# A gated delta rule's state update: contraction over a unit's 128 rows with keys set to nought in the other chunk's rows, instead of over the chunk's own 64 rows

## The chip, the cores and the metric

The kernel runs on one core of one Trainium2 chip, as one program with one launch. The metric is the device time in microseconds. Matrix products run on TensorE (PE in the profile; its weight loads are a row of their own, PEld), elementwise work on VectorE (DVE), ScalarE (ACT) and GpSimd (POOL); SyncE (SP) issues the DMAs.

## The reference

Two layers of a decoder trunk over 1024 tokens with 1024 channels. Each layer normalises its input, projects it once, feeds three token mixers that read the same projection, gates each branch, and adds an output projection to the input. A last RMS norm follows. Only the first mixer is touched here: the gated delta rule with 4 heads of 128 channels in chunks of 64 tokens.

```
def step(state, inp):
    q_n, k_n, u_n, w_n, g_n, a_n = inp
    v_new = u_n - einsum('bhck,bhkv->bhcv', w_n, state)
    o = einsum('bhck,bhkv->bhcv', q_n * exp(g_n)[..., None], state) + einsum('bhij,bhjv->bhiv', a_n, v_new)
    g_last = g_n[..., -1]
    state = state * exp(g_last)[..., None, None] + einsum(
        'bhck,bhcv->bhkv', k_n * exp(g_last[..., None] - g_n)[..., None], v_new)
    return state, o
```

The last einsum, the state update, contracts over the tokens c of one chunk (64 of them). The keys in it are decayed by exp(g_last - g).

The other two mixers are a latent attention with 8 heads and a gated linear recurrence (RG-LRU) of 512 channels.

## The kernel before

The work of a layer has three stages. In the first (phase_a) the input projection is done column tile by column tile: in_tile loads a weight block of 128x1024, splits it into an exact high and low part (wst, whi by DVE on L111, wlo by POOL on L112), and does 48 products of 128x512 with them (L121, L122, L123), into a PSUM tile pbig. Beside these products runs the delta rule. The second stage is the RG-LRU and the first half of the output projection, the third is the attention and the other half.

The delta rule works on two pairs of heads, one after the other, so that there are four scans in all (two layers by two pairs). The tokens of a pair stand in eight units of 128, and a unit holds two chunks, one in partitions 0 to 63 and one in 64 to 127. Four quads of four (unit, head) matrices are prepared (gdn_prep, products on L415, L421, L426, L434) and then scanned (gdn_scan). For each chunk the scan does, in this order: the products of the state S with w and q for both heads (L459, into the PSUM tile pS), the new values vn = uu - pS (DVE, L92, 64 rows), the products of the decayed keys kd with vn for both heads (L463, into pD), and the new state for both heads (DVE, L89, tile S). A copy of pS's other rows (ACT, L466) keeps q's part. At the end of a unit come the products of the decayed attention with vn for both heads (L471). All these are plain float32, and each such product is two records on PE and two on PEld, so that a chunk's L463, with two heads, is four records. There are 2 x 2 x 8 x 2 = 64 chunks, 64 visits to L463.

The line L463 takes only the chunk's own rows of kd and vn (`mine`, 64 of 128), so that its matmul uses 64 rows of the array; the profile marks it 64*128. Everything else in the scan is 128*128. The attention has one other 64*128 product, L749.

The keys kd are made in gdn_prep by POOL, one instruction of 128x128 per (unit, head), from ktok and a column of dec (L412, which the profile books on the helper's line L95). dec holds exp(g_last - g) per token, each row with its own chunk's g_last. kd has two buffers of 128x512, one per quad. POOL works in order and also makes bk, bv and wlo.

A scheduler sets the order of the instructions on each engine from the order of the program, priorities and its own model of durations. in_tile's products have a low priority: they fill the gaps of the scan. An engine then works strictly through that order.

Of the kernel before, what the change touches and what calls it, by code (L numbers as in the profile page):

```python
# [9 lines left out]
F32 = mybir.dt.float32  # L10
# [7 lines left out]
L = 2  # L18
# [4 lines left out]
# Columns of a layer's parameter tile [128, NPAR].  # L23
# [15 lines left out]
# Columns of the constant tile [128, NCON].  # L39
# [10 lines left out]
# Indices of the input projection's column tiles.  # L50
# [13 lines left out]
class Trunk:  # L64
# [7 lines left out]
    @contextmanager  # L72
    def prio(self, d):
        """Instructions that the scheduler prefers less (d > 0) or more (d < 0)."""
        self.tc.cur_priority += d
        yield
        self.tc.cur_priority -= d
# [19 lines left out]
    def load_w(self, src, nk, cols, eng=None, pool=None):  # L97
        """A float32 weight block [128, nk, cols] as its exact float32r parts."""
# [17 lines left out]
    def mm3(self, out, pairs):  # L116
        """out = sum over (ah, al, bh, bl) of a.T @ b, each in three float32r products."""
# [7 lines left out]
    def split(self, hi, lo, x, eng=None):  # L125
        """x as exact float32r parts: hi is x rounded, lo the rest."""
        self.nc.scalar.copy(hi, x)  # L127
        (eng or self.nc.vector).tensor_tensor(lo, x, hi.bitcast(F32), ALU.subtract)  # L128

# [1 line left out]
    def in_tile(self, l, *ms):  # L131
        """The first of the column tiles ms; the others wait for their call. All by halves of the tokens."""
# [13 lines left out]
    def conv(self, y, p, w, bias=None):  # L146
        """Causal depthwise conv of width 4 along the free axis, from PSUM."""
# [7 lines left out]
    def silu2(self, out, z):  # L155
        """out = 2 silu(z), as z (1 + tanh(z / 2))."""
        self.act(out, z, AF.Tanh, scale=0.5)
        self.stt(out, out, 1.0, z, ALU.add, ALU.mult)
# [5 lines left out]
    def newton(self, r, x):  # L164
        """One Newton step of r towards x ** -0.5; x is overwritten."""
# [5 lines left out]
    def add_squares(self, alloc, acc, x, eng):  # L171
        """acc + x * x (acc is None at first)"""
# [7 lines left out]
    def rms_bcast(self, alloc, accs, n, ch, tag, fine=False):  # L180
        """1 / sqrt(mean of squares + eps), on every partition, from the sum of accs over their channels."""
        nc = self.nc
        r = alloc("rb")
        if not fine:
            # brings Ln's table in while the sums are still under way
# [15 lines left out]
    def norm_half(self, alloc, xs, accs, n, gain, tag, share=False):  # L201
        """h = rmsnorm(x) for one half of the tokens, into self.hh, self.hl."""
# [12 lines left out]
    def gates(self, l):  # L215
# [16 lines left out]
        # beside them the RG-LRU's parameters  # L232
# [22 lines left out]
        dec = pa.tile([128, 32], F32, name="dec")  # L255
        for c in range(2):
            q = slice(64 * c, 64 * c + 64)
            self.tt(dec[q], gs[q, 32 + 32 * c : 64 + 32 * c], gc[q], ALU.subtract)
        self.act(dec, dec, AF.Exp)
# [10 lines left out]
    def gdn_qkv(self, l, pr, kind, hd, P):  # L270
# [22 lines left out]
        # squared norms of q, columns (unit, head)  # L293
# [7 lines left out]
    def combos(self, q):  # L301
        """The four (unit, head) of quad q: index, unit, head of the pair, columns."""
        return [(c, 2 * q + c // 2, c % 2, slice(c * 128, c * 128 + 128)) for c in range(4)]

    def gdn_tok(self, pr, P):
        """k and v by token, and the pair's factors per token."""
# [14 lines left out]
        # inverse norms: 1 / sqrt(sum + eps), of vectors that are twice the reference's  # L321
# [9 lines left out]
        # v is held doubled  # L331
# [7 lines left out]
    def gdn_pre(self, pr, P, q):  # L339
        """-A and the decayed attention of one quad; the diagonal blocks go out by DRAM."""  # L340
# [31 lines left out]
    def blocks(self, dram, b):  # L372
        """Diagonal block b (32 x 32) of each of a pair's sixteen 128 x 128 matrices."""
        return bass.AP(dram.tensor, dram.offset + b * (32 * 2048 + 32), [[128, 16], [2048, 32], [1, 32]])

    def gdn_inverse(self, pr):
        """(I + A)^-1 of the 32 x 32 diagonal blocks, one block per partition, and its transpose."""
# [18 lines left out]
    def gdn_prep(self, pr, P, q):  # L396
        """The quad's triangular inverse, applied to v and k."""
# [8 lines left out]
        kd = pa.tile([128, H2], F32, name="kd", tag="kd", bufs=2)  # L406
        for c, u, hd, cs in self.combos(q):
# [4 lines left out]
            self.gts(kd[:, cs], P["ktok"][q][:, cs], self.dec[:, gj : gj + 1])  # L412
# [14 lines left out]
        for hd in range(2):  # L427
            # w of a unit's two chunks around that unit's q
# [10 lines left out]
    def gdn_scan(self, pr, P, q):  # L439
        nc, pa = self.nc, self.pa  # L440
        if q == 0:
            P["S"] = [pa.tile([128, 128], F32, name="S", tag="S", bufs=4) for _ in range(2)]
            for s in P["S"]:
                nc.gpsimd.memset(s, 0.0)
        S, uu, kd = P["S"], P["u"][q], P["kd"][q]
        # the output takes the place of the decayed attention
        o = P["attn"][q]
        for ul in range(2):
            u = 2 * q + ul
            vn = pa.tile([128, 256], F32, name="vn", tag="vn", bufs=2)  # L450
            oq = pa.tile([128, 256], F32, name="qs", tag="qs", bufs=2)
            for par in range(2):
# [8 lines left out]
                for hd, cs, gj in hs:  # L461
                    cq = slice((ul * 2 + hd) * 128, (ul * 2 + hd) * 128 + 128)
                    nc.tensor.matmul(pD[:, cs], kd[mine, cq], vn[mine, cs], start=True, stop=True)  # L463
# [13 lines left out]
    def gdn_norm(self, pr, P):  # L477
        """The output's RMS norm, its gate and its way out; q's inverse norm and 128^-0.5 with them."""
# [31 lines left out]
    def gate_tile(self, l, m, dst, z=None):  # L510
        """2 silu of a column tile, to DRAM"""
# [7 lines left out]
    def lru(self, l):  # L519
        nc, pa, par = self.nc, self.pa, self.par  # L520
        st, res = [], []
        for m in range(4):
# [22 lines left out]
            # 1 - a^2 = tanh(-log a) (1 + a^2)  # L545
# [112 lines left out]
    def rope(self, x, n, s):  # L658
        """Rotary embedding of one half of the tokens; x may be in PSUM."""
# [13 lines left out]
    def attn_q_rope(self, l, pr, res):  # L673
        """q's rotary part of two heads: parts stacked as [hi; lo] per head."""
# [30 lines left out]
    def attn_v(self, l, pr, V):  # L705
        """v of two heads: per two token blocks, [128, (block, head, 128)]."""
# [470 lines left out]
```

## Time and profile before

| | |
|---|---|
| median of three runs | 2239.93 us (2239.56, 2239.93, 2247.45) |
| profiled execution, first to last instruction | 2240.5 us |
| PE busy | 2143.5 us (96%), 10380 records |
| DVE, ACT, POOL busy | 1321.0, 880.7, 705.6 us |
| granted TensorE clock, mean | 0.984 of full |

The profile is of one execution. Besides the span of its instructions it gives no second time for that execution; the span stands 0.6 us above the median of the runs, so that the two can be compared directly. Busy times of PE are unions of pipelined records, whose ends are modelled: what a product costs is read from the distance between starts, not from its duration.

### The profile page before, as it was taken

How to read it: one execution, taken by the hardware profiler on the slowest of the kernel's cores; microseconds unless marked ns; L12 is line 12 of the kernel's file. 1: busy time of each engine (PE TensorE's matmuls, PEld its weight loads, DVE VectorE, ACT ScalarE, POOL GpSimd, SP SyncE). 2: the span in 40 equal slices, each digit the busy share in tenths (PEclk: the TensorE clock that was granted, in tenths of full speed). 3: DMA queues.
4: the chain of work that ended last, by engine and by line, in shares of the span. 5: the costliest groups of instructions: out<-in, count | busy, mean ns of one | idle time of the engine just before them, and what ended most of it. 6: DMA issues, size and time to landing. Idle time of an engine off the chain costs nothing. (4 is left out here: it accounts for less than half of the span.)

```text
span 2240.5 us, 28710 instructions
## 1 busy us (share of the span) xinstructions
PE 2143.5 (96%) x10380; PEld 1695.7 (76%) x10380; DVE 1321.0 (59%) x2496; ACT 880.7 (39%) x1784; POOL 705.6 (31%) x712
## 2 busy tenths in 40 slices
PE   7999999999899999999989999999998999999997
PEld 4788877787677777777668888788777877777774
DVE  6546547545833766666664575483467247666666
ACT  5241254135611544443533313522375025443535
POOL 3222222323632333232242222322336323232322
PEclk9999999999999999999999999999999999999999
DMA  4223113412253024326321331134213520325172
GB/s 149 71 78 111 53 57 99 135 41 85 94 186 100 20 79 143 122 88 198 129 78 38 109 97 36 57 99 128 72 60 122 169 82 30 121 88 175 43 226 99
DMA packets 135101, 222.06 MB, mean 99 GB/s; under 512 B 37808, under 2 KB 60336, under 8 KB 134960
## 3 DMA queue, kind: packets, MB, share of 16 engines
q1 hardware_dynamic: 134960, 220.24, 30.6%
q8 instruction: 82, 1.34, 0.3%
q14 instruction: 59, 0.48, 0.1%
HBM read 147.31 MB, written 72.88 MB: 98 GB/s over the span
## 5 line engine op out<-in xcount | busy, mean ns | idle before, releaser
L112 POOL TENSOR_TENSOR wlo<-wst,whi 128x1024 fp32r<-128x1024 f32 (+3 forms) x196 | 316.2, 1614 | 903.6 <-DVE whi L111 308.8
L121 PE MATMUL pbig<-h,whi 128*128 128x512 f32 x1216 | 486.4, 400 | 9.2 <-ACT h L127 6.2
L123 PE MATMUL pbig<-h,wlo 128*128 128x512 f32 x1216 | 486.5, 400 | 4.0 <-POOL wlo L112 4.0
L122 PE MATMUL pbig<-h,whi 128*128 128x512 f32 x1216 | 485.8, 399 | 2.1 <-DVE h L128 1.0
L121 PEld LDWEIGHTS pbig<-h,whi 128*128 128x128 f32 x1216 | 231.7, 191 | 56.6 <-ACT h L127 7.0
L123 PEld LDWEIGHTS pbig<-h,wlo 128*128 128x128 f32 x1216 | 231.7, 191 | 50.8 <-POOL wlo L112 5.3
L122 PEld LDWEIGHTS pbig<-h,whi 128*128 128x128 f32 x1216 | 231.4, 190 | 50.2 <-POOL h L128 3.3
L86 ACT ACTIVATE P<-pS,mx,scq 128x512 f32<-128x512 f32 (+1 forms) x192 | 128.1, 671 | 158.9 <-DVE mx L89 88.2
L111 DVE CAST whi<-wst 128x1024 fp32r<-128x1024 f32 x92 | 76.9, 836 | 150.2 <-PE pbig L122 118.4
L95 POOL TENSOR_SCALAR P<-P,mx 128x128 f32<-128x128 f32 (+6 forms) x112 | 80.6, 720 | 231.0 <-DVE mx L766 186.9
L109 ACT CAST whi<-wst 128x256 fp32r<-128x256 f32 (+2 forms) x104 | 46.3, 447 | 231.3 <-DMA wst<-in_w_uq 105.2
L127 ACT CAST pth<-pstp 128x512 fp32r<-128x512 f32 x192 | 91.3, 479 | 93.2 <-PE pstp L795 93.2
L755 DVE TENSOR_REDUCE mx<-pS 128x1 f32<-128x512 f32 (+1 forms) x192 | 106.6, 555 | 24.3 <-PE pS L749 17.1
L128 DVE TENSOR_TENSOR ptl<-pstp,pth 128x512 fp32r<-128x512 f32 x192 | 105.1, 554 | 23.9 <-ACT pth L127 23.2
L86 ACT ACT_TABLE_LOAD x81 | 103.9, 1283 | 2.4 <-PEq L1169 0.7
L795 PE MATMUL pstp<-con,P 128*128 128x128 f32 x576 | 98.7, 278 | 3.4 <-DVE P L770 3.4
L121 PE MATMUL pspj<-lh,whi 128*128 128x512 f32 x208 | 88.1, 424 | 6.1 <-DVE k L128 5.5
L92 DVE TENSOR_TENSOR xt<-pspj,xt 128x512 f32<-128x512 f32 x96 | 66.3, 690 | 46.7 <-PE pspj L123 40.8
L795 PEld LDWEIGHTS pstp<-con,P 128*128 128x128 f32 x576 | 71.2, 141 | 25.0 <-DVE P L770 4.8
L749 PE MATMUL pS<-kl,qr 64*128 64x512 f32 (+1 forms) x192 | 85.1, 443 | 0.0
L123 PE MATMUL pspj<-lh,wlo 128*128 128x512 f32 x208 | 82.4, 396 | 0.6 <-POOL wlo L112 0.6
L122 PE MATMUL pspj<-ll,whi 128*128 128x512 f32 x208 | 82.4, 396 | 0.0
(267 smaller groups left out, 4565.5 us busy)
## 6 DMA issues: line engine op xcount, KB each, us to landing
wst<-in_w_in SPq DMA_DIRECT2D x76, 512.0 KB, 3.6
x<-xt SPq DMA_DIRECT2D x128, 256.0 KB, 3.2
xt<-x SPq DMA_DIRECT2D x112, 256.0 KB, 3.4
mzd<-z SPq DMA_DIRECT2D x16, 512.0 KB, 3.6
wst<-in_w_o SPq DMA_DIRECT2D x16, 512.0 KB, 3.6
mz<-mzd SPq DMA_DIRECT2D x32, 256.0 KB, 2.8
wst<-in_w_o SPq DMA_DIRECT2D x64, 128.0 KB, 2.1
xk<-x SPq DMA_DIRECT2D x32, 256.0 KB, 4.3
```

Source lines behind the costliest of these rows:

```text
L86: self.nc.scalar.activation(out, in_, func, **kw)
L95: self.nc.gpsimd.tensor_scalar(out, a, s, 1.0, ALU.mult, ALU.mult)
L111: nc.vector.tensor_copy(hi[:, :n], st[:, :n])
L112: (eng or nc.gpsimd).tensor_tensor(lo[:, :n], st[:, :n], hi[:, :n].bitcast(F32), ALU.subtract)
L121: nc.tensor.matmul(out, ah, bh, start=(j == 0), stop=False)
L122: nc.tensor.matmul(out, ah, bl, start=False, stop=False)
L123: nc.tensor.matmul(out, al, bh, start=False, stop=(j == n - 1))
L127: self.nc.scalar.copy(hi, x)
L128: (eng or self.nc.vector).tensor_tensor(lo, x, hi.bitcast(F32), ALU.subtract)
L749: nc.tensor.matmul(out, qr[sb][0:64, qs], self.kl[0:64, a:e], start=False, stop=True)
L755: nc.vector.tensor_reduce(mx[:, j : j + 1], S[j], AX.X, ALU.max, negate=True)
L795: nc.tensor.transpose(tp[:, qi * 128 : qi * 128 + 128], P[qi][:, kb * 128 : kb * 128 + 128], self.ident)
```

## The change

The scan's state update takes all 128 rows of a unit. So that the other chunk's tokens add nothing, there are now two tiles of decayed keys per quad, one per chunk, each with nought in the other chunk's rows:

- dec becomes [128, 2, 32], is set to nought first (DVE), and each half is written by its own exp on ACT (two of 64x32 instead of one of 128x32).
- kd becomes a list of two tiles; POOL makes 8 instead of 4 instructions of 128x128 per quad. kd has four buffers instead of two, so that it is as deep as before, in quads.
- vn is now two tiles that live through a pair's whole scan, set to nought once at its start (POOL), since a product now also reads rows that belong to the chunk that is not yet computed (old values times nought).
- the product on L463 (now L468) takes kd[par] and vn whole.

The number of products is the same. Comments and docstrings are gone from the file, and lines move by up to five: L459, L463, L471 are now L464, L468, L476; L415, L421, L426, L434 are L418, L424, L429, L437; the memsets of the scan (L444) are L449.

```
-        dec = pa.tile([128, 32], F32, name="dec")
+        dec = pa.tile([128, 2, 32], F32, name="dec")
+        nc.vector.memset(dec, 0.0)
         for c in range(2):
             q = slice(64 * c, 64 * c + 64)
-            self.tt(dec[q], gs[q, 32 + 32 * c : 64 + 32 * c], gc[q], ALU.subtract)
-        self.act(dec, dec, AF.Exp)
+            self.tt(dec[q, c], gs[q, 32 + 32 * c : 64 + 32 * c], gc[q], ALU.subtract)
+            self.act(dec[q, c], dec[q, c], AF.Exp)
...
-        kd = pa.tile([128, H2], F32, name="kd", tag="kd", bufs=2)
+        kd = [pa.tile([128, H2], F32, name="kd", tag="kd", bufs=4) for _ in range(2)]
...
-            self.gts(kd[:, cs], P["ktok"][q][:, cs], self.dec[:, gj : gj + 1])
+            for par in range(2):
+                self.gts(kd[par][:, cs], P["ktok"][q][:, cs], self.dec[:, par, gj : gj + 1])
...
             P["S"] = [pa.tile([128, 128], F32, name="S", tag="S", bufs=4) for _ in range(2)]
-            for s in P["S"]:
+            P["vn"] = [pa.tile([128, 256], F32, name="vn", tag="vn", bufs=2) for _ in range(2)]
+            for s in P["S"] + P["vn"]:
                 nc.gpsimd.memset(s, 0.0)
...
-            vn = pa.tile([128, 256], F32, name="vn", tag="vn", bufs=2)
+            vn = P["vn"][ul]
...
-                    nc.tensor.matmul(pD[:, cs], kd[mine, cq], vn[mine, cs], start=True, stop=True)
+                    nc.tensor.matmul(pD[:, cs], kd[par][:, cq], vn[:, cs], start=True, stop=True)
```

On PE the order of instructions is the same as before in both layers, except in the first layer from the middle of its second scan to the RG-LRU. The queue of PE there, in the second scan of the first layer, before (z, tf and bv belong to the preparation of the next quad, pbig to the filling products):

```order
L121 MATMUL pbig<-h,whi 128x512
L122 MATMUL pbig<-h,whi 128x512
L421 MATMUL pspr<-z,mt 128x128 x4
L463 MATMUL pssc<-vn,kd 128x128 x2
L123 MATMUL pbig<-h,wlo 128x512
L121 MATMUL pbig<-h,whi 128x512
L426 MATMUL pspr<-tf,bk 128x128 x4
L434 MATMUL pspr<-bv,tf 128x128 x4
L459 MATMUL pssc<-S,wq 128x128 x2
L122 MATMUL pbig<-h,whi 128x512
```

And the same place of the changed kernel:

```order
L121 MATMUL pbig<-h,whi 128x512
L122 MATMUL pbig<-h,whi 128x512
L123 MATMUL pbig<-h,wlo 128x512
L424 MATMUL pspr<-z,mt 128x128 x4
L468 MATMUL pssc<-vn,kd 128x128 x2
L121 MATMUL pbig<-h,whi 128x512
L122 MATMUL pbig<-h,whi 128x512
L429 MATMUL pspr<-tf,bk 128x128 x4
L437 MATMUL pspr<-bv,tf 128x128 x4
L464 MATMUL pssc<-S,wq 128x128 x2
```

One filling product has moved ahead of the preparation's product of z; the products are the same ones.

POOL's queue at the start of a pair (here the first of the first layer), before:

```order
L112 TENSOR_TENSOR wlo<-wst,whi 128x1024 x7
L95 TENSOR_SCALAR kd<-ktok,dec 128x128 x8
L112 TENSOR_TENSOR wlo<-wst,whi 128x1024
L95 TENSOR_SCALAR bk<-ktok,br2e 128x128
L95 TENSOR_SCALAR bv<-vtok,br 128x128 x2
```

The same place of the changed kernel:

```order
L112 TENSOR_TENSOR wlo<-wst,whi 128x1024 x7
L95 TENSOR_SCALAR kd<-ktok,dec 128x128 x13
L112 TENSOR_TENSOR wlo<-wst,whi 128x1024
L95 TENSOR_SCALAR kd<-ktok,dec 128x128 x3
L95 TENSOR_SCALAR bk<-ktok,br2e 128x128
L95 TENSOR_SCALAR bv<-vtok,br 128x128 x2
```

The keys of two quads are 16 instructions instead of 8, and the split of one weight block (wlo) stands behind 13 of them instead of 8.

POOL's queue towards the end of a first pair's scan, before:

```order
L95 TENSOR_SCALAR kd<-ktok,dec 128x128 x4
L112 TENSOR_TENSOR wlo<-wst,whi 128x1024
L95 TENSOR_SCALAR bk<-ktok,br2e 128x128 x4
L95 TENSOR_SCALAR bv<-vtok,br 128x128 x4
L95 TENSOR_SCALAR kd<-ktok,dec 128x128 x4
L112 TENSOR_TENSOR wlo<-wst,whi 128x1024 x2
L95 TENSOR_SCALAR at<-at,ms 128x128 x16
```

The same place of the changed kernel:

```order
L95 TENSOR_SCALAR kd<-ktok,dec 128x128 x8
L112 TENSOR_TENSOR wlo<-wst,whi 128x1024
L95 TENSOR_SCALAR bk<-ktok,br2e 128x128 x4
L95 TENSOR_SCALAR bv<-vtok,br 128x128 x4
L95 TENSOR_SCALAR kd<-ktok,dec 128x128 x8
L112 TENSOR_TENSOR wlo<-wst,whi 128x1024
L449 MEMSET vn 128x256 x2
L112 TENSOR_TENSOR wlo<-wst,whi 128x1024
L95 TENSOR_SCALAR at<-at,ms 128x128 x16
```

Beside the doubled keys, the memsets of the next pair's vn, which must wait for the last products that read this pair's vn, stand between two splits of weight blocks.

## Rows read from the trace of the kernel before

**Rows 1.** The page: PE's busy tenths in 40 slices of 56 us.

```profile
PE   7999999999899999999989999999998999999997
```

**Rows 2.** Windows: four stretches of 60 us, one in each scan, their sum.

```profile
sum 240.00, PE 235.96 PEld 195.21 DVE 122.69 ACT 83.56 POOL 66.30; mean PE 58.99 PEld 48.80 DVE 30.67 ACT 20.89 POOL 16.57
```

**Rows 3.** Groups by line and form: busy us, mean ns | idle before, releaser.

```profile
L463 PE MATMUL pssc<-vn,kd 64*128 64x128 f32 x256 | 45.9, 300 | 0.0
L459 PEld LDWEIGHTS pssc<-S,wq 128*128 128x128 f32 x256 | 37.9, 194 | 2.9
L95 POOL TENSOR_SCALAR kd<-ktok,dec 128x128 f32<-128x128 f32 x64 | 22.7, 373 | 69.1 <-PE pssc L463 41.5 <-ACT ktok L315 27.6
```

**Rows 4.** Timeline of PE in the first scan: start us, us, engine, line.

```profile
268.42 0.39 PE L122 MATMUL pbig<-h,whi 128*128 128x512 f32 x1
268.65 0.60 PE L459 MATMUL pssc<-S,wq 128*128 128x128 f32 x4
...
269.32 0.39 PE L121 MATMUL pbig<-h,whi 128*128 128x512 f32 x1
...
269.79 0.40 PE L123 MATMUL pbig<-h,wlo 128*128 128x512 f32 x1
270.11 0.71 PE L463 MATMUL pssc<-vn,kd 64*128 64x128 f32 x4
...
271.10 0.40 PE L122 MATMUL pbig<-h,whi 128*128 128x512 f32 x1
```

**Rows 5.** Timeline of PE: a visit with L471 behind it; eight records elsewhere.

```profile
266.44 0.40 PE L122 MATMUL pbig<-h,whi 128*128 128x512 f32 x1
266.77 0.71 PE L463 MATMUL pssc<-vn,kd 64*128 64x128 f32 x4
...
268.19 0.39 PE L121 MATMUL pbig<-h,whi 128*128 128x512 f32 x1
...
440.85 1.05 PE L421 MATMUL pspr<-z,mt 128*128 128x128 f32 x8
...
441.98 0.40 PE L121 MATMUL pbig<-h,whi 128*128 128x512 f32 x1
```

**Rows 6.** Timeline of PE in the attention, around its 64-row product L749.

```profile
743.67 0.33 PE L806 MATMUL pspo<-pth,vh 128*128 128x384 f32 x1
743.84 0.33 PE L807 MATMUL pspo<-pth,vl 128*128 128x384 f32 x1
744.10 0.50 PE L749 MATMUL pS<-kl,qr 64*128 64x512 f32 x1
744.53 0.45 PE L808 MATMUL pspo<-ptl,vh 128*128 128x384 f32 x1
```

**Rows 7.** Timeline of PE and DVE: the chain of one chunk and a half.

```profile
253.35 0.71 PE L463 MATMUL pssc<-vn,kd 64*128 64x128 f32 x4
...
254.10 0.60 DVE L89 SCALAR_TENSOR_TENSOR S<-S,ge,pssc 128x128 f32<-128x128 f32 x2 [1.15 <-PE pssc L463]
...
254.78 0.61 PE L459 MATMUL pssc<-S,wq 128*128 128x128 f32 x4
...
255.43 0.42 DVE L92 TENSOR_TENSOR vn<-uu,pssc 64x256 f32<-64x256 f32 x1 [0.73 <-PE pssc L459]
...
256.02 0.71 PE L463 MATMUL pssc<-vn,kd 64*128 64x128 f32 x4
```

**Rows 8.** Timeline: a first head's product beside the second head's state.

```profile
264.37 0.39 PE L459 MATMUL pssc<-S,wq 128*128 128x128 f32 x2
...
264.56 0.34 DVE L89 SCALAR_TENSOR_TENSOR S<-S,ge,pssc 128x128 f32<-128x128 f32 x1
```

**Rows 9.** Timeline of POOL: a pair's start, and behind a pair's scan.

```profile
132.63 2.40 POOL L112 TENSOR_TENSOR wlo<-wst,whi 128x1024 fp32r<-128x1024 f32 x1
145.42 0.37 POOL L95 TENSOR_SCALAR bk<-ktok,br2e 128x128 f32<-128x128 f32 x1 [10.38 <-DVE br L332]
...
307.62 2.41 POOL L112 TENSOR_TENSOR wlo<-wst,whi 128x1024 fp32r<-128x1024 f32 x1 [17.78 <-PE pbig L123]
```

## The prediction

> **What bounds the kernel now.** I read the page first, then windows over the four scans, then PE's timeline inside them, and DVE's and POOL's beside it. PE is busy nearly throughout; the slices under 9 tenths lie at the start, the end, and around the change from the RG-LRU to the output projection and from one layer to the next [rows 1]. In the four stretches taken inside the scans PE is busy 235.96 of 240 us, so 4 us of 240 are idle, while DVE has 122.69 and POOL 66.30 us of work [rows 2]. So the scan is no chain that PE waits for: the filling products are laid into its gaps, and whatever PE spends on a visit to L463 is on the path. The question is then what a visit costs PE, and whether the chain through DVE still fits when PE needs less.
>
> **PE: what the 64 rows cost.** The products themselves are the same number, 256 records or 64 visits of four [rows 3], and the same columns. What differs is seen in the distance between starts. Around L459, four records of 128 rows between filling products, the start of the filling product ahead of it lies at 268.42 and that of the second one behind it at 269.32: 0.90 us. Around L463, four records of 64 rows in the same setting, it is 269.79 to 271.10: 1.31 us [rows 4]. The difference is 0.41 us. Where L471 stands directly behind L463 the stretch is 266.44 to 268.19, 1.75 us; eight records of 128 rows with the next filling product take 440.85 to 441.98, 1.13 us, and the step of the filling product ahead is 0.23 (268.19 to 268.42), 1.36 us in all: a difference of 0.39 us [rows 4, 5]. Part of this lies ahead of L463 (0.32 from the product before it, where 0.23 is the rule) and the rest inside and behind it.
>
> Could it be the wait for vn instead? L463 has to wait for vn, which DVE has just made, and the profile books some idle time so. Two things speak against it. The stretch has the same length whether vn was done long before or just before. And the attention's product of 64 rows, which has no vn, shows the same: the step ahead of it is 0.26 us where one of 384 columns takes 0.17, and its own step of 512 columns is 0.43 where the rule is 0.23 [rows 4 to 6]. That is 0.29 us for one visit of a single record, with the step behind it not counted. So I take it as the price of going from 128 rows to 64 and back, which the change removes at all 64 visits. About three quarters of them (48, counted in the timeline) come behind a filling product, the others behind the preparation's 128x128 products; I take the mean of the two differences, 0.40, for all: 64 x 0.40 = 25.6 us off PE.
>
> The bounds of this: nothing, if it is the wait after all, and 64 x 0.41 = 26.2 us from the longer row; the visits behind the preparation's products may have a little more to give.
>
> On loads the Trainium skill has a rule that speaks against the change: in "TensorE: Matmul & The Clock Gate", Part 3, The mechanism, it says that weight loads overlap with matmuls in flight only when the row group differs, and 128 rows next to 128 rows share all groups. Here no such thing shows at L459, whose four loads last 0.194 us each, 0.78 together, in a stretch of 0.90 in which two filling products take 0.46. By the page's rule the sum would turn into a loss, by the rows it is the gain above; I go by the rows, and the loss stands below as a rival.
>
> **DVE: does the chain still fit?** From L463's start the new state of both heads is done after 1.35 us (253.35 to 254.70), and the next L459 starts at 254.78, 0.08 later; PE fills that time with three products [rows 7]. About 38 of the 64 legs are as tight as this. On PE that leg is 1.43 us now, and with 128 rows it becomes 1.43 - (0.40 - 0.09) = 1.12, since 0.09 of the 0.40 is saved ahead of the visit. The chain shrinks less: four records last 0.60 from the first start to the last end instead of 0.71 [rows 4], so that the state of the second head is done after about 1.25 and that of the first, 0.30 earlier, after 0.95. The first head's product needs only the first head's state: at 264.37 it starts while DVE has the second head's state still ahead of it, 264.56 [rows 8]. So it can start at 0.95 + 0.08 = 1.03, ahead of 1.12. The second head's product stands two records behind; the eight of rows 5 take 1.13 less a filling product's 0.23, 0.11 each, so that it is due at 1.34, and its state is ready for it at 1.25 + 0.08 = 1.33. It fits, barely. In the other leg, L459 to L463, vn ends at 255.85 and L463 starts at 256.02, 0.17 later [rows 7]; with the 0.09 off, 0.08 is left, which is as tight as the tightest start seen. I take 1.5 us of such waits in all. If the next L459 had to wait for both heads, each tight leg would lose 1.33 - 1.12 = 0.21, 38 of them 8.0 us; and if the vn leg kept its 0.09 in the some 24 legs that have only three products in them, 2.2 more.
>
> **POOL: the doubled keys.** 64 more instructions at 0.373 us are 23.9 us of POOL [rows 3], which has 66.30 of 240 us of work there [rows 2]. What they can do is come late themselves, or hold up wlo, for which filling products would then wait. At a pair's start 16 take 6.0 us instead of 3.0; POOL there has 10.38 us idle ahead of bk [rows 9], which covers it, and the one wlo in front of which five more of them stand (at most 1.9 us, and part of that is a gap in which POOL waited for ktok) belongs to a filling product some microseconds later. In the scan a batch is 3.0 instead of 1.5 us, once per quad and two quads ahead of its use. The memsets of vn (eight of 128x256, none of which the trace has; between nothing and twice a key's 0.373 each, so 0.8 for the pair of them) wait for the end of the scan before, with a wlo behind them; that wlo waits for its buffer until 307.62 anyway [rows 9], later than the scan's last product. I take nothing for POOL; with the cover gone altogether it would be all of the 23.9 us. DVE's two memsets and the two further exps of ACT come where nothing waits for dec yet: nothing, at most half a microsecond.
>
> **Moved work.** PE's order differs only in the first layer from the second scan on; the same products stand there, one filling product earlier or later, and the RG-LRU's small products are dealt out otherwise. I take nothing, and 2 us either way. The attention is untouched and only shifts.
>
> **Sum.** 2240.5 - 25.6 + 1.5 = 2216.4 us against the profiled execution, which lies 0.6 above the median of the runs; so I forecast 2216, with 2211 to 2221 as this case's own range.
>
> **Rivals.** *The chain takes over.* The scan is left waiting for the state of both heads: 25.6 - 8.0 - 2.2 = 15.4 us gained, 2224. For it speaks how tight rows 7 are, against it rows 8. Chance 0.16.
>
> *Given back behind the scans.* After each layer's second scan the RG-LRU keeps the vector engines busy and PE falls to 8 tenths [rows 1]. If that stretch starts from something that does not move with PE, the gain of two of the four scans is lost: 12.8 left, 2227. Against it: its inputs are products at the end of PE's own queue. Chance 0.07.
>
> *It does not do what it says.* The longer stretch at L463 is vn's release after all, or a product's way through the array costs the same in either shape: no gain, 2240. The attention's rows speak against it. Chance 0.06.
>
> *Slower: loads in the open.* With 128 rows on both sides the loads of kd can no longer go beside the products before them. A visit would then cost 0.90 + 4 x 0.194 = 1.68 instead of 1.31, 64 x 0.37 = 23.7 us more: 2264. It decides from 0.10 us per load in the open, where the gain of 0.41 is used up. L459 has the same shape and neighbours and shows nothing of it [rows 3, 4]. Chance 0.04. POOL holding up filling products by all its 23.9 us would leave next to no gain (2238), with 0.03.
>
> **How the numbers follow.** The forecast's own case has 0.64. A change under 0.5% (11.2 us) is about what a measurement of this kernel cannot tell from none. The forecast and the chain's case are beyond that, and the given-back case half: 0.64 + 0.16 + 0.04 + some of what is unnamed, 0.86 for faster; 0.09 for the same (the other half, the case without effect, POOL); 0.05 for slower. The range runs from 2210, which is the longer row at every visit (26.2) with 4 us more for the visits behind the preparation, to 2228, which takes in the chain's case and the given-back case.
>
> **What would show it.** In the profile after, the stretch around the state update's four records, marked 128*128, should be about 0.90 to 0.95 us between filling products and 1.36 with the attention product behind; PE's busy time in total should be lower by 20 to 26 us, its idle time in the scans about as before; kd on POOL should count 128 at 0.37 us; the scans should each be some 6 us shorter and everything behind them start earlier by that. It would be wrong if the stretch stayed at 1.3 us, if PE's idle time ahead of L459 (L464) grew by 0.1 to 0.2 us a visit, or if filling products waited for wlo in the scans.

## The result, and the profile after

| | before | after |
|---|---|---|
| median | 2239.91 us (2239.56 to 2247.45, 4 runs) | 2223.31 us (2222.12 to 2225.87, 4 runs) |
| profiled execution, first to last instruction | 2240.5 us | 2222.4 us |
| PE busy | 2143.5 us | 2124.1 us |

The ratio is 0.9923 with a 95% interval of 0.9907 to 0.994: 16.6 us faster, where 24 were forecast. The time lies inside the range of 2210 to 2228, which took in two of the rivals, 7 us above the forecast and outside the 2211 to 2221 of the forecast's own case. The page of the kernel after, busy us of each engine:

```profile
PE 2124.1 (96%) x10380; PEld 1684.2 (76%) x10380; DVE 1324.3 (60%) x2498; ACT 881.5 (40%) x1786; POOL 729.5 (33%) x784
```

PE is busy for 19.4 us less with the same 10380 records, POOL for 23.9 us more. The groups by line and form of the kernel after, which answer to [rows 3] (busy us, mean ns | idle before, releaser):

```profile
L464 PE MATMUL pssc<-S,wq 128*128 128x128 f32 x256 | 42.3, 285 | 0.0
L468 PE MATMUL pssc<-vn,kd 128*128 128x128 f32 x256 | 41.3, 284 | 0.1
L468 PEld LDWEIGHTS pssc<-vn,kd 128*128 128x128 f32 x256 | 34.8, 191 | 10.0 <-DVE vn L92 5.5 <-issue 3.1
L464 PEld LDWEIGHTS pssc<-S,wq 128*128 128x128 f32 x256 | 34.6, 190 | 7.4 <-issue 4.6 <-DVE S L89 0.4
L95 POOL TENSOR_SCALAR kd<-ktok,dec 128x128 f32<-128x128 f32 x128 | 45.5, 375 | 46.5 <-PE pssc L468 24.4 <-ACT ktok L317 22.0
```

The state update is now marked 128*128, and POOL makes 128 keys of 0.375 us. PE books next to no idle time at either product (0.0 and 0.1 us), but its load queue does: 7.4 us ahead of L464's loads, where it was 2.9 ahead of the same loads on L459 [rows 3]. That is a trace of what went missing, and a reader who looks at PE's row alone does not see it. The queue's idle time is no measure of the loss, though: ahead of the update's own loads it fell, to 10.0 us from what this row of the kernel before has.

```profile
L463 PEld LDWEIGHTS pssc<-vn,kd 64*128 64x128 f32 x256 | 33.5, 188 | 19.5 <-DVE vn L92 13.9 <-issue 3.1 <-ACT qs L466 0.7
```

PE's timeline of the kernel after, first at a visit between filling products, then at one with L476 behind it; they answer to [rows 4, 5]:

```profile
255.77 0.40 PE L122 MATMUL pbig<-h,whi 128*128 128x512 f32 x1
256.01 0.61 PE L468 MATMUL pssc<-vn,kd 128*128 128x128 f32 x4
256.37 0.48 PE L123 MATMUL pbig<-h,wlo 128*128 128x512 f32 x1
256.69 0.39 PE L121 MATMUL pbig<-h,whi 128*128 128x512 f32 x1
256.92 0.39 PE L122 MATMUL pbig<-h,whi 128*128 128x512 f32 x1
257.15 0.68 PE L464 MATMUL pssc<-S,wq 128*128 128x128 f32 x4
257.59 0.48 PE L123 MATMUL pbig<-h,wlo 128*128 128x512 f32 x1
...
268.22 0.40 PE L122 MATMUL pbig<-h,whi 128*128 128x512 f32 x1
268.45 0.69 PE L468 MATMUL pssc<-vn,kd 128*128 128x128 f32 x4
268.98 0.61 PE L476 MATMUL pspr<-vn,at 128*128 128x128 f32 x4
269.35 0.48 PE L123 MATMUL pbig<-h,wlo 128*128 128x512 f32 x1
269.66 0.40 PE L121 MATMUL pbig<-h,whi 128*128 128x512 f32 x1
```

The first stretch, 255.77 to 256.69, is 0.92 us, as forecast (0.90 to 0.95, before 1.31). The second, 268.22 to 269.66, is 1.44 us where 1.36 was forecast and 1.75 stood before. In it the four records of L468 take 0.53 us to the next start, in the first stretch 0.36, and L464, which is four records of the same shape, takes 0.44 (257.15 to 257.59) where the kernel before has 0.37 (254.78 in [rows 7] to 255.15 in the row below). The loads say why. The load queue of the kernel after:

```profile
255.78 0.65 PEld L468 LDWEIGHTS pssc<-vn,kd 128*128 128x128 f32 x4
...
257.12 0.52 PEld L464 LDWEIGHTS pssc<-S,wq 128*128 128x128 f32 x4 [0.24 <-issue]
...
268.43 0.52 PEld L468 LDWEIGHTS pssc<-vn,kd 128*128 128x128 f32 x4 [0.25 <-DVE vn L92]
```

And, of the kernel before, the load of L459 in the chain of [rows 7], and the product behind L459:

```profile
254.56 0.64 PEld L459 LDWEIGHTS pssc<-S,wq 128*128 128x128 f32 x4
255.15 0.48 PE L123 MATMUL pbig<-h,wlo 128*128 128x512 f32 x1
```

Before, L459's load starts 0.22 us ahead of its product (254.56 and 254.78): it lies beside the filling product before it. After, L464's starts 0.03 ahead (257.12 and 257.15), so that most of the first load of 0.19 us comes after the product's own start. What is loaded, wq and kd, is ready long before; but in this trace the load waits for the product's other operand. The first head's state (a state takes 0.344 us on average) ends at 254.44 before and 256.99 after, and the load starts 0.12 and 0.13 us later. In the operations booked to the line there is a semaphore wait in the load queue (PEldq) at that place; before and after:

```profile
L459 PEldq EVENT_SEMAPHORE  x1: 51/51/51, 254.5 to 254.5; - x1
```

```profile
L464 PEldq EVENT_SEMAPHORE  x1: 51/51/51, 257.0 to 257.0; - x1
```

The one other wait there is for ACT, whose copy of the last pS had ended at 253.54 before and 256.23 after. So the chain state to product is not 0.08 us, as the forecast had it from the second head's state, but 0.12 to the load and another 0.22 to hide the load. Counted over the four scans:

| four records of 128 rows in one piece | before | after |
|---|---|---|
| L459/L464, load more than 0.15 us ahead | 40, step 0.361 us | 4, step 0.364 us |
| L459/L464, load less than 0.1 us ahead | none | 36, step 0.436 us |
| L468, filling product behind, load over 0.15 us ahead | (64 rows) | 17 of 20, step 0.363 us |
| L468, L476 behind, load less than 0.1 us ahead | (64 rows) | 28 of 28, step 0.528 us |
| L468, preparation ahead and L476 behind, load 0.11 us ahead | (64 rows) | 4 of 4, step 0.447 us |

The step is the distance from the group's first start to the next product's start; all but the last row have a filling product ahead. (The few groups whose two heads stand apart are left out of the table.) A group whose load is held takes 0.07 to 0.08 us longer.

The scans, from the first start of L459 (L464) to the last of L471 (L476), took 59.77, 58.13, 64.12 and 59.24 us before, and 55.89, 54.46, 55.73 and 54.23 after: 3.9, 3.7, 8.4 and 5.0 us less. The third and the fourth scan before held a stretch at a low clock (see the last section), so I do not read their 8.4 and 5.0 us. The first scan has the same products in the same order in both kernels. Its distances between starts, added up by kind over the whole scan (a preparation's group of eight right ahead of the state update is in the first row):

| first scan, us | before | after | difference |
|---|---|---|---|
| into the state update (16) | 8.04 | 6.78 | -1.26 |
| the state update's own (16) | 10.21 | 7.04 | -3.17 |
| L471/L476's own (7) | 3.45 | 2.73 | -0.72 |
| into L459/L464 and their own | 13.09 | 13.92 | +0.83 |
| into the preparation's products | 5.67 | 6.25 | +0.58 |
| filling products | 19.31 | 19.17 | -0.14 |
| sum | 59.77 | 55.89 | -3.88 |

Four times 3.88 is 15.5 us, against 16.6 in the medians; four times the second scan's 3.67 would be 14.7.

### The profile page after: what moved, and what is told of

It reads as the page before. It is cut to its first block, busy times and chain, and to the rows that moved or that the text cites. A ratio compares the mean times of both kernels' runs of the same rounds, so it can differ in the third digit from the quotient of the medians.

```text
span 2222.4 us, 28794 instructions
## 1 busy us (share of the span) xinstructions
PE 2124.1 (96%) x10380; PEld 1684.2 (76%) x10380; DVE 1324.3 (60%) x2498; ACT 881.5 (40%) x1786; POOL 729.5 (33%) x784
## 5 line engine op out<-in xcount | busy, mean ns | idle before, releaser
L754 PE MATMUL pS<-kl,qr 64*128 64x512 f32 (+1 forms) x192 | 84.3, 439 | 0.0
```

Source lines behind the costliest of these rows:

```text
L754: nc.tensor.matmul(out, qr[sb][0:64, qs], self.kl[0:64, a:e], start=False, stop=True)
```

## The experiments

Each was run beside the kernel before on the same chip; ratios are to that kernel (medians 2243.68 us beside e1 to e4, 2242.96 beside e5 to e8, 2242.35 beside e9 to e11), with 95% intervals.

**e1: the doubled keys alone.** The changed kernel with the product taken from 64 rows.

```
-    matmul(pD[:, cs], kd[par][:, cq], vn[:, cs])
+    matmul(pD[:, cs], kd[par][mine, cq], vn[mine, cs])
```

> The changed kernel with one thing undone: the state update takes the chunk's own 64 rows of kd and vn again. The doubled keys on POOL, the memsets and the lasting vn stay. Theory (all of the gain is PE's change between 64 and 128 rows, POOL's extra work is hidden): as before the change, 2240 us, between 2237 and 2242; four records of the update 0.64 us from start to next start as before. Rival (the part of the forecast gain that is missing, some 8 us, went to POOL's doubled keys): 2246 to 2250.

Measured: 1.0007 [0.9989, 1.0024], 2247.22 us. POOL made all 128 keys, and PE had the old form:

```profile
L468 PE MATMUL pssc<-vn,kd 64*128 64x128 f32 x256 | 45.7, 299 | 0.0
L95 POOL TENSOR_SCALAR kd<-ktok,dec 128x128 f32<-128x128 f32 x128 | 45.4, 375 | 52.2 <-PE pssc L468 30.2 <-ACT ktok L317 22.0
```

The time itself lies in the rival's 2246 to 2250, but on this chip the kernel before took 2243.68 us too, and the ratio makes it 2241.5 on the scale of the expectation, inside the theory's 2237 to 2242. The 23.9 us of POOL cost nothing that the interval shows (between 2.5 us gained and 5.4 lost), and without the product's 128 rows there is no gain.

**e2: 128 rows without doubled keys.** One key tile per quad; the nought in the other chunk's rows is left out, so that the state also takes in keys that don't belong there.

```
-    kd = [pa.tile(..., bufs=4) for _ in range(2)]
+    kd = [pa.tile(..., bufs=2)]
...
-    for par in range(2):
-        self.gts(kd[par][:, cs], P["ktok"][q][:, cs], self.dec[:, par, gj : gj + 1])
+    self.gts(kd[0][:, cs], P["ktok"][q][:, cs], self.dec[:, 0, gj : gj + 1])
...
-    matmul(pD[:, cs], kd[par][:, cq], vn[:, cs])
+    matmul(pD[:, cs], kd[0][:, cq], vn[:, cs])
```

> The changed kernel with one tile of keys per quad instead of two: POOL makes as many keys as before, and the 128-row product takes them without nought in the other chunk's rows (left out: the masking, so the state also holds the other chunk's keys times values that don't belong there). Theory (POOL hidden): as the changed kernel, 2220 to 2226 us. Rival (POOL's doubled keys took the missing 8 us): 2213 to 2217.

Measured: 0.990 [0.9878, 0.9921], 2221.87 us. The interval overlaps the changed kernel's (0.9907 to 0.994); the ratios differ by 5 us, give or take 6, and 0.990 of 2239.9 us is 2218, between the theory's range and the rival's. So the time alone leaves open whether half of the keys cost POOL nothing or a few us; what bounds POOL is e1. But the profile of e2 has the same 36 groups of L464 with a held load as the changed kernel, so that these waits do not come from POOL.

**e3 and e4: the chain cut, before and after.** The scan's first product takes a constant tile of noughts instead of the state, in the kernel before (e3) and the changed one (e4), so that L459 or L464 waits for no new state. What is left out is the state's way back into the scan.

```
+    P["Z"] = pa.tile([128, 128], F32, name="zs", tag="zs", bufs=2)
+    nc.gpsimd.memset(P["Z"], 0.0)
...
-    matmul(pS[:, cs], P["wq"][hd][...], S[hd])
+    matmul(pS[:, cs], P["wq"][hd][...], P["Z"])
```

> The kernel before, with the scan's first product taking a constant tile of noughts instead of the state (left out: the state's way back into the scan; all instructions stay). No L459 waits for the state any more. Theory (in the kernel before PE fills all the chain's waits already): 2236 to 2241 us, next to no gain. Rival (the scan of the kernel before is held by the chain too): under 2234. It is the base of the next run.

> The changed kernel with the same cut: the scan's first product takes a constant tile of noughts. Theory (the change takes 0.40 us off each of 64 visits, and some 8 us of that are given back because the chain over the state and vn is now too tight for the weight loads to run ahead): 2214 to 2219 us, that is 22 to 26 us under the run with the cut in the kernel before, where the change itself brought 16.6. Rival (a visit is only worth 0.26 us): the same 16 to 18 us between the two cut kernels as between the two whole ones, 2221 to 2224.

Measured: e3 1.0031 [1.0012, 1.005], 2251.88 us; e4 0.9903 [0.9885, 0.992], 2223.97 us. Between the two the change is worth 27.9 us instead of 16.6, some 23 to 34 by the two intervals: about what the forecast has without waits (25.6). The scans in the profiles became 4.8, 5.5, 4.9 and 5.4 us shorter instead of some 4. That fits the chain as the place of the loss, but it is no proof. e3 is 8 us slower than the kernel before, which neither its theory nor its rival had. e4 lies in its rival's 2221 to 2224 as a time and in its theory's 2214 to 2219 as a ratio (2218 of 2239.9 us); it is only some 3 to 5 us faster than the changed kernel, so that most of what the 27.9 us have over 16.6 comes from e3. Without the link the scheduler lays 70 instead of 104 filling products into the first scan, only 4 groups of L464 are left behind a filling product (44 in the changed kernel), and only 20.6 of the 27.9 us are in the scans.

**e5 and e6: the attention's 64-row product.** The same idea at L749 (L754 after): kl's rows 64 to 127 are set to nought once per layer and the product takes all rows; e5 on the changed kernel, e6 on the kernel before.

```
+    nc.vector.memset(kl[64:128].bitcast(F32), 0.0)
...
-    matmul(out, qr[sb][0:64, qs], self.kl[0:64, a:e], start=False, stop=True)
+    matmul(out, qr[sb][:, qs], self.kl[:, a:e], start=False, stop=True)
```

> The changed kernel with the same trick at the other product of 64 rows, the attention's (192 products): the low part of the rotary keys gets nought in rows 64 to 127 and the product takes all 128 rows; nothing else changes and no vn is near it. Theory (going from 128 rows to 64 and back costs PE some 0.3 to 0.4 us at each visit, whatever the product waits for): 192 x 0.30 to 0.40 = 58 to 77 us, 2146 to 2166. Rival (the price was the wait for vn in the scan): 2221 to 2225. Rival (the attention is held by softmax work on DVE and ACT, and PE's gain is given back): 2190 to 2215.

> The kernel before, with only the attention's product made 128 rows. Theory: the same 58 to 77 us as on the changed kernel, 2163 to 2182, since the two places don't meet. Rival (the two changes share a cover, so that one alone brings less or more than beside the other): the difference to the kernel before is more than 8 us away from the one that the same edit makes on the changed kernel.

Measured: e5 0.9708 [0.9691, 0.9725], 2178.12 us; e6 0.9808 [0.979, 0.9826], 2199.57 us. e5 is the version that beats both kernels: 48 us below the changed kernel on the same chip (e8), 65 below the kernel before. The price of going to 64 rows and back shows at a product that has no vn near it, so that the rival of the wait for vn (2221 to 2225) is out. But both gains are below the expected 58 to 77 us: 48 on the changed kernel, 43 on the kernel before. These two are 5 us apart, within the 8 us from which e6's rival would have spoken of a shared cover. PE's timeline of this kernel in the attention (from e10, the same kernel again), which answers to [rows 6]:

```profile
739.95 0.40 PE L754 MATMUL pS<-kp,qr 128*128 128x512 f32 x1
740.18 0.40 PE L755 MATMUL pS<-kl,qr 128*128 128x512 f32 x1
740.41 0.23 PE L812 MATMUL pspo<-pth,vh 128*128 128x128 f32 x1
```

The product of 512 columns takes 0.23 us to the next start, where it was 0.43 before [rows 6]. Over the visits in two stretches of the attention (720 to 1060 and 1820 to 2100; 162 of the 192 in e8, 167 in e5) the three steps from the group of products ahead to the second group behind went from 0.975 to 0.643 us on average: 0.33 each, 64 us over all 192. 48 arrived. In 740 to 1040 PE is busy for 297.41 of 300 us in e8, the changed kernel:

```profile
740.00:1040.00 300.00, 297.41 (x1473) 228.40 (x1472) 201.79 (x470) 136.66 (x332) 97.34 (x109) 1.00 0.32 102
```

and in the attention's version e5 (the columns are the stretch, its length, busy us of PE, PEld, DVE, ACT and POOL with their counts, PE's clock, the DMA share and GB/s):

```profile
740.00:1040.00 300.00, 291.44 (x1570) 244.21 (x1569) 210.64 (x491) 140.59 (x342) 99.27 (x113) 1.00 0.37 118
```

More records fit into the same time, and 8.6 us of it are idle instead of 2.6. So in the attention too part of the gain turns into waits; with the second layer's (1840 to 2140: 11.2 instead of 2.6) some 14.5 us. In the stretch shown 4.1 of e5's 8.6 us end with DVE's ptl, 2.5 with DVE's P and 1.7 with ACT's P, where e8 has 1.7 for DVE's P and 0.9 for ACT's. These are tiles of the softmax: e5's other rival, that this work holds PE, is part of the truth, though its 2190 to 2215 was too slow.

**e7: vn per head, and e8: the changed kernel again.** vn is made by two instructions, one per head, so that the first head's product need not wait for both.

```
-    self.tt(vn[mine, :], uu[mine, ul * 256 : ul * 256 + 256], pS[mine, :256], ALU.subtract)
+    for hd, cs, gj in hs:
+        c0 = ul * 256 + hd * 128
+        self.tt(vn[mine, cs], uu[mine, c0 : c0 + 128], pS[mine, cs], ALU.subtract)
```

> The changed kernel with vn made per head (two DVE instructions of 64x128 instead of one of 64x256), so that the first head's update product can start before the second head's vn. Theory (the chain's last tenth of a microsecond holds back loads): if the scheduler uses it, up to 4 us less than the changed kernel, 2219 to 2224; the second instruction's fixed time on DVE eats some of it. Rival (the chain is no bound): no change or slower by DVE's extra work, 2223 to 2227.

> The changed kernel itself, beside the others on their chip, for comparison: 2220 to 2227 us, 0.990 to 0.994 of the kernel before.

Measured: e7 0.9904 [0.9883, 0.9925], 2221.23 us; e8 0.9927 [0.9913, 0.9941], 2226.39 us. The intervals overlap. The loads moved as they should. The load queue of e7 at a visit with the decayed attention's product (L478 here) behind it:

```profile
270.25 0.56 PEld L470 LDWEIGHTS pssc<-vn,kd 128*128 128x128 f32 x4
```

and PE there:

```profile
270.40 0.60 PE L470 MATMUL pssc<-vn,kd 128*128 128x128 f32 x4
270.85 0.61 PE L478 MATMUL pspr<-vn,at 128*128 128x128 f32 x4
```

The load starts 0.15 us ahead of its product, and the four records take 0.45 us instead of 0.53. Of 25 whole groups of this kind 19 have the load over 0.1 us ahead, with a step of 0.442 us on average, and six have it 0.03 to 0.10 ahead, with 0.477; without the edit it was 0.023 ahead and 0.528. That shows the held load as the cause of the long step. It is worth 28 x 0.08 = 2.2 us at most. The four scans of e7 are 215.94 us together and those of e8 219.40, but they hold 380 filling products instead of 387, of some 0.24 us each; about 1.8 us are left, which is near what was to be had and too little for the medians to tell. L464's loads stayed held (35 whole groups, step 0.433).

**e9: both, and e10: e5 again.** e9 joins the edits of e5 and e7.

> The changed kernel with two edits together: vn made per head (as in e7_vn_heads) and the attention's product contracted over 128 rows (as in e5_attn_128). Theory that the chain still holds the scans back by its waits: e7 gave 0 to 5 us and the attention 48 us; they lie in different stages, so the sum is 2170 to 2178 us, a ratio of 0.968 to 0.971 to the kernel before. Rival, that the gain of vn per head is nothing more than a different order in one profiled execution: the time is that of e10_attn_again, within 1.5 us.

> The kernel of e5_attn_128 once more, on the chip of e9_both: 2178 us or a ratio of 0.969 to 0.9725 by every theory, as the measure for e9_both.

Measured: e9 0.9723 [0.9696, 0.9749], 2178.7 us; e10 0.9705 [0.9681, 0.9729], 2176.6 us. The two cannot be told apart: if vn per head brings its 2 us, the medians do not show it (they differ by 2.1 us the other way). The expected 2170 to 2178 was missed by a little, and the rival's 1.5 us as well; this pair decides nothing.

**e11: only the first chunks at 128 rows.**

```
-    matmul(pD[:, cs], kd[par][:, cq], vn[:, cs])
+    rows = slice(0, 128) if par == 0 else mine
+    matmul(pD[:, cs], kd[par][rows, cq], vn[rows, cs])
```

> The changed kernel in which only the visits of a unit's first chunk take 128 rows, and those of its second chunk 64 rows, as before the change. Theory that a visit's price depends on what stands around it and that the visits with the attention's product behind them (all of them second chunks) gave the least: of the 32 first-chunk visits some 20 gain 0.38 us and 12 about 0.55, some 14 us off PE, less 1 to 3 us of waits that the tighter chain takes; the time is 2227 to 2231 us if the second chunks gave little. Rival, that each visit gives the same: half of the 16.6 us, 2231 to 2232 us. Rival, that the missing 9 us are lost only when all chunks are quick: 2226 us or less, 14 us gained by half the visits.

Measured: 0.9966 [0.995, 0.9982], 2235.89 us; of the 2239.9 us of the kernel before that ratio is 2232.3. The gain, 7.6 us (4 to 11), is half of the whole. That is nearest to the first rival, 2231 to 2232; my theory, that the second chunks had given little (2227 to 2231), is not favoured but lies partly within the interval (2229 to 2236). The second rival, 2226 or less, is out: the loss is not one that begins only when all chunks are quick. One piece of this kernel's timeline has both kinds of leg side by side, PE first:

```profile
267.01 0.71 PE L469 MATMUL pssc<-vn,kd 64*128 64x128 f32 x4
...
268.89 0.60 PE L464 MATMUL pssc<-S,wq 128*128 128x128 f32 x4
269.25 0.47 PE L123 MATMUL pbig<-h,wlo 128*128 128x512 f32 x1
...
270.26 0.61 PE L469 MATMUL pssc<-vn,kd 128*128 128x128 f32 x4
270.63 0.47 PE L121 MATMUL pbig<-h,whi 128*128 128x512 f32 x1
...
271.40 0.68 PE L464 MATMUL pssc<-S,wq 128*128 128x128 f32 x4
271.84 0.47 PE L121 MATMUL pbig<-h,whi 128*128 128x512 f32 x1
```

and the loads of the two L464:

```profile
268.66 0.64 PEld L464 LDWEIGHTS pssc<-S,wq 128*128 128x128 f32 x4
...
271.37 0.52 PEld L464 LDWEIGHTS pssc<-S,wq 128*128 128x128 f32 x4 [0.24 <-issue]
```

Behind the slow visit of 64 rows the load of L464 runs 0.23 us ahead and its four records take 0.36; behind the quick one it runs 0.03 ahead and they take 0.44. Over the kernel, of the whole groups of L464 between filling products, the load ran ahead in all 20 behind a visit of 64 rows and was held (less than 0.1 us ahead) in 16 of 20 behind one of 128; with all chunks quick 36 of 40 are held, before the change none. So the loss comes leg by leg, and what decides is the visit ahead.

## Why the prediction was right, and where it was not

**The price of 64 rows: right.** The state update's rows cost PE what the forecast read off the distance between starts. A visit between filling products fell from 1.300 to 0.918 us over the 20 of them (three with a held load), 0.38 each where 0.40 was taken. In e1 the gain goes with the rows, and e5 shows the same price in a place without vn. So the visit's length was not vn's release, and the rival without effect is out. The Trainium skill, in "TensorEngine Tiling (Array Packing)", Key Properties, says that a change of the tiling mode drains the engine; it gives no price, and the 0.38 us here and 0.33 in the attention agree with it as far as they go.

**The loads of 128 rows next to 128 rows: right.** The rival of 2264 us would have had four loads a visit in the open. They lie beside the products before them wherever they may start early: 17 groups with a step of 0.363 us hold four loads of 0.19, 0.76 together. The Trainium skill's rule in "TensorE: Matmul & The Clock Gate", Part 3, The mechanism, that loads overlap only where the row group differs, is not what this trace shows. What the same page says elsewhere, in Part 2, Step-by-step, that a load is also pulled ahead where it goes to the background weight buffer, agrees with these rows, though no row shows the buffer itself. But loads were the matter after all, in another way, and that is the step below.

**DVE, "It fits, barely": this step failed.** It took 0.08 us from the end of a state to the product behind it, which was the distance from the second head's state to L459 [rows 7], and put it behind the first head's state: 0.95 + 0.08 = 1.03, ahead of PE's 1.12. The product waits for the first head's state, as the forecast argued from [rows 8], but what that state releases is the load, 0.12 us later, and the load needs 0.22 more to be hidden. The same sum with these is 0.95 + 0.12 + 0.22 = 1.29, against 1.12: not barely in time but 0.17 late, and the part of it that shows is 0.07 per leg; why no more, no run shows. It costs 36 x 0.075 = 2.7 us at L464, and at the 28 visits ahead of L476, where vn releases the load, 28 x 0.08 = 2.2 us. The 1.5 us of waits were mis-sized.

**The sum, with what was measured.** By the table of the first scan, times four: the visits gave 4 x 5.15 = 20.6 us instead of 25.6, of which 2.2 are the held loads of L468 and the other 2.8 a price of rather 0.36 to 0.38 than 0.40. The waits took 4 x 1.27 = 5.1 us instead of 1.5: 2.7 of held loads at L464, and the rest mostly ahead of the preparation's products (+0.58 in the first scan). 20.6 - 5.1 = 15.5 us.

Of the 0.58, 0.21 stand ahead of the scan's first L418, which waits for the DMA of tq: 1.37 us to its start before, 1.59 after, but 1.43 in e8, the same kernel, so that this part is not the change's for sure. The rest is the same step again, at one L424 behind z and one L429 behind tf, both made by DVE. The L429, in the kernel before (as L426) and after:

```profile
277.89 0.39 PE L121 MATMUL pbig<-h,whi 128*128 128x512 f32 x1
278.12 1.05 PE L426 MATMUL pspr<-tf,bk 128*128 128x128 f32 x8
```

```profile
278.46 0.40 PE L121 MATMUL pbig<-h,whi 128*128 128x512 f32 x1
278.79 0.97 PEld L429 LDWEIGHTS pspr<-tf,bk 128*128 128x128 f32 x8 [0.37 <-issue]
278.82 1.13 PE L429 MATMUL pspr<-tf,bk 128*128 128x128 f32 x8
```

tf ends at 278.67, the load starts 0.12 later, and the product stands 0.36 behind the one ahead of it instead of 0.23. In e1, with all of POOL's keys but 64 rows, it is 0.24, in e2, with half of the keys and 128 rows, 0.36: it goes with the rows. In the four scans ten of L424 and L429 start so late, where one did before, and each loses some 0.2 us, 0.13 ahead of it and 0.08 in its own group: 1.8 us for the nine.

**The rival "The chain takes over" had the size (15.4 us, 2224) but not the mechanism.** It wanted L464 to wait for both heads. In the kernel after L464 starts at 257.15; DVE's row of that moment, which answers to the state's row in [rows 7], has the second state still under way:

```profile
256.65 0.61 DVE L89 SCALAR_TENSOR_TENSOR S<-S,ge,pssc 128x128 f32<-128x128 f32 x2 [0.95 <-PE pssc L468]
```

Both states end at 257.26, so that only the first was waited for. That the chain through the state is the place of the loss rests on the loads, on e11 (the same leg held or not by the visit ahead of it) and, weakly, on e3 and e4.

**POOL: right; the moved work: no sign of a cost.** kd took 0.375 us each, and PE's waits for wlo stayed at 4.0 us; e1 bounds the whole at 5.4 us, and e2 does not contradict it.

**What would show it.** The stretch between filling products came out as forecast, the one ahead of L476 0.08 too long, PE's busy time fell by 19.4 instead of 20 to 26 us, the scans by some 4 instead of 6. The sign that I had named for a failure, idle time of PE ahead of L464, did not appear, although the failure was there: a held load lengthens the record of the product behind it (0.68 instead of 0.61 for the four, mean 285 instead of 278 ns) and is booked as idle time of the load queue.

## What to carry to other kernels

Look for products of fewer rows than their neighbours: if the missing rows can be filled with nought for little, the distance between starts says what that gives, here 0.33 to 0.38 us per visit, and it gave 16.6 us in the scan and 48 in the attention, each less than the price times the visits, because the work around it had waits of its own. When a link from a vector engine to a product is to become tighter, count to the weight load and not to the product, since in this trace the load waits with its product and wants 0.22 us of lead besides. And read the load queue's idle time beside PE's own.

## What the runs showed of the hardware that was not expected

The wait stands ahead of the load of wq, an operand that has long been ready, and not only ahead of the product that needs the state: a load held 0.03 us ahead of its product costs 0.07 to 0.08 us on a group of four.

The clock falls in stretches that are not the same from kernel to kernel. In the third scan of the kernel before (columns as above; the third from the end is PE's clock):

```profile
1340.00:1350.00 10.00, 7.47 (x39) 6.28 (x38) 2.26 (x5) 1.60 (x4) 2.80 (x8) 0.77 0.33 103
1350.00:1360.00 10.00, 10.00 (x62) 8.69 (x60) 3.64 (x10) 2.77 (x9) 2.80 (x8) 0.89 0.17 52
```

and ahead of the first scan of the kernel after:

```profile
55.00:60.00 5.00, 2.85 (x15) 2.26 (x13) 4.48 (x6) 2.40 (x2) 2.35 (x1) 0.89 1.04 331
60.00:65.00 5.00, 5.00 (x13) 3.94 (x13) 3.61 (x6) 1.79 (x4) 0.00 (x0) 0.50 0.45 148
```

PE was idle for 2.5 of the 10 us in the one place and for 2.15 of the 5 us ahead of the lowest row in the other, and the granted clock was 0.77 on average over those 10 and 0.50, the lower of its levels (1.2 GHz), over the 5 behind, with fewer records in the same busy time (13 in 5 us). But such idle time does not settle it. The same place of e10 has the same 2.15 us and no fall:

```profile
55.00:60.00 5.00, 2.85 (x17) 2.18 (x16) 4.46 (x7) 2.40 (x2) 2.36 (x1) 1.00 1.03 347
60.00:65.00 5.00, 5.00 (x24) 4.13 (x23) 3.74 (x7) 1.80 (x4) 0.00 (x0) 1.00 0.49 152
```

And in the fourth scan of the kernel before the clock fell although PE had been busy all of the 10 us ahead:

```profile
1550.00:1560.00 10.00, 10.00 (x67) 8.22 (x65) 4.29 (x13) 3.76 (x15) 4.21 (x13) 1.00 0.36 134
1560.00:1570.00 10.00, 10.00 (x61) 8.96 (x61) 3.76 (x13) 4.91 (x9) 1.64 (x5) 0.83 0.11 27
```

Such a stretch costs 1 to 4 us here: the third scan before took 4.35 us more than the first, the fourth 1.1 more than the second, and the first scan after began 3 us later (245.63 and 242.59; in e10, without the fall, 242.60). That is up to about a fourth of this change's gain, so a single scan of a single profile is no measure of it, and the scans had to be compared with one another first.
